# Layer 0's first adaLN columns summed by TensorE instead of GpSimd, h from x in two VectorE operations, rotary constants made in layer 0's MLP

## The chip, the cores and the metric

The kernel runs on one core of one Trainium2 chip. The metric is the time of one execution on the device in microseconds (us), the median of several runs. The engines are TensorE (PE; its weight loads are shown as PEld), VectorE (DVE), ScalarE (ACT), GpSimd (POOL) and SyncE (SP, which issues most transfers). Each engine takes its instructions in the order in which the built program holds them and waits where an operand is not there yet.

## The reference

A trunk of two layers on a sequence of 1024 tokens of 1024 features, all in fp32. Layer 0 mixes tokens by gated linear attention, layer 1 by differential attention with rotary positions; a squared-ReLU MLP follows each. Ahead of each mixer and MLP the input is normed and modulated by six vectors that depend on the condition `c` (adaLN). What the change touches:

```python
ang = positions.astype(f32)[..., None] * inv_freq
cos = jnp.cos(ang); sin = jnp.sin(ang)                      # used in layer 1
c_act = jax.nn.silu(c)
mod = c_act @ ada_w[i] + ada_b[i]                           # 1024 -> 6 x 1024
shift_t, scale_t, gate_t, shift_c, scale_c, gate_c = split(mod, 6)
h = rmsnorm(x, norm_g[i, 0]) * (1.0 + scale_t) + shift_t    # input of the mixer
q, k, v, r, a_lr = split(h @ w_in)                          # layer 0
```

## The kernel before, in words

Features lie on the 128 partitions in eight tiles k, tokens in the free dimension in two halves of 512. Every fp32 product is made of three products of rounded operands: `split` (L114 on ACT, L115 on DVE) writes a tile as `hi` plus `lo`, and `mm3` multiplies hi by hi, hi by lo and lo by hi (L118, L119, L120).

The begin works on the first half of the tokens. SP fetches x token by token (`xt`); ACT sums squares (L260) and `rsqrt_cols` makes 1/rms per token; PE transposes x into feature tiles (`tr`, L344), ACT copies them out (`xT`, L345), and PE spreads 1/rms over the partitions (`bc`, L164). DVE multiplies the two into `xn` (L346).

Only the first 2048 of 6144 adaLN columns, shift and scale of the mixer, are needed now. They come in four blocks (`blk`): 256 columns of shift and the same 256 of scale, for all eight k, as a tile `aw` of [128, 4, 2, 256] per half of the k (four buffers). The vector-matrix product is made in two steps: first acc[p, column] = sum over k of w[p, k, column] * cact[p, k], in which ACT makes the products for k = 0, 1, 2 (L332), POOL adds two of them (L334), and DVE adds the other five as chained multiply-adds (L336); then PE sums acc over the partitions, by four products with a column of ones (`st`, L356). DVE adds the bias (L360, L363: `mod`) and makes the gain (L361: `gs`). From these each block gives the h of two k tiles: ACT writes `h_hi` = g * xn + shift (L368), DVE the same in fp32 (`ht`, L369) and `h_lo` = ht - h_hi (L370). PE then takes up the products of the new h tiles with the weights of v and the gate rank (`pv`, 272 columns), q (`pq`, 512) and k (`pk`, 512); when all eight tiles are through, it transposes the rank part (`tra`, L431), on which the decay and the rest of the layer hang.

The order on each engine is set by a scheduler when the program is built, from its own estimate of the durations; `in_order` pins the transfers of the begin on SP's queue. The rotary constants (`diff_constants`, L1310 on) are made in the begin: some 25 small DVE operations that depend on each other, one sine on ACT between two table loads. They are used in layer 1 only.

Layer 0's MLP consists of an inner part, in which DVE and ACT make sums and splits of the weights (`ws`, `whi`, `wlo`) and of parts of the hidden (`sum`, `inner`), and of `outer`, which multiplies by the second matrix.

Of the kernel before, what the change touches and what calls it, by code (L numbers as in the profile page):

```python
# [10 lines left out]
F32 = mybir.dt.float32  # L11
# [4 lines left out]
AF = mybir.ActivationFunctionType  # L16
ALU = mybir.AluOpType
# [65 lines left out]
def trunk(ctx: ExitStack, tc, a, out):  # L83
    nc = tc.nc
    pe, act, dve, pool = nc.tensor, nc.scalar, nc.vector, nc.gpsimd


    const = ctx.enter_context(tc.tile_pool(name="const", bufs=1))
    wsp = ctx.enter_context(tc.tile_pool(name="wsp", bufs=5))
    wraw = ctx.enter_context(tc.tile_pool(name="wraw", bufs=2))  # L90
    hp = ctx.enter_context(tc.tile_pool(name="hp", bufs=2 * KT))
# [6 lines left out]

    dve.memset(const.tile([P, 40], F32, name="gap"), 0.0)
    ident = const.tile([P, P], F32, name="ident")  # L100
    make_identity(nc, ident)
    ones_col = const.tile([P, 1], F32, name="ones_col")
    dve.memset(ones_col, 1.0)
    colsT = const.tile([P, NROWS], F32, name="colsT")
    adabT = const.tile([P, 96], F32, name="adabT")
    cact = const.tile([P, KT], F32, name="cact")
# [54 lines left out]
    def broadcast(bc, cols, n):  # L161

        for j in range(n):
            pe.matmul(out=bc[:, j * P:(j + 1) * P], lhsT=cols[:, j:j + 1].broadcast_to([P, P]),  # L164
                      rhs=ident, start=True, stop=True)
# [86 lines left out]
    win = a["gla_w_in"][0]  # L252
    xn = [hp.tile([P, HT], F32, name="xn", tag="hhi") for _ in range(KT)]
    xT = [hp.tile([P, HT], F32, name="xT", tag="hlo") for _ in range(KT)]
# [8 lines left out]
    with tc.tile_pool(name="xa", bufs=4, reuse_waits="tile") as xa, \  # L263
# [30 lines left out]
        pe.transpose(out=st0[:, 2, 16:16 + KT], in_=pos_f, identity=ident[:KT, :KT])  # L294
        pos = pro.tile([P, KT], F32, name="pos")
        dve.tensor_copy(out=pos, in_=st0[:, 2, 16:16 + KT])
# [9 lines left out]
        pe.matmul(out=st0[:, 2, 40:42], lhsT=ones_col[:DH, :].broadcast_to([DH, P]), rhs=lp, start=True, stop=True)  # L306
        le = pro.tile([P, 2], F32, name="le")
        act.activation(out=le, in_=st0[:, 2, 40:42], func=AF.Exp)

        xt = []  # L310
        for j in range(4):
            t = xa.tile([P, D], F32, name="xt", tag="xt")
# [4 lines left out]
        token_rms(xt, pro2, ssq, rstd, pro.tile([P, D], BF16, name="junk"))  # L317
        cos, sin, neglam, gsub, cmin = diff_constants(tc, const, pro, pos, le, colsT)
        w_v0, w_q0, w_k0 = [], None, None
        aw = a["ada_w"][0][:, 0:2 * D].rearrange("(k p) (j n) -> p k j n", p=P, j=2)  # L320
        for blk in range(4):
            c0 = blk * 256
            acc = pro2.tile([P, 2, 256], F32, name="acc", tag="acc")
            for kq in range(2):
                w = pro2.tile([P, 4, 2, 256], F32, name="aw", tag="aw", bufs=4)
                for j in (1, 0):
                    in_order(nc.sync.dma_start(out=w[:, :, j, :], in_=aw[:, 4 * kq:4 * kq + 4, j, c0:c0 + 256]))
                for i in range(4):
                    k = 4 * kq + i
                    if k < 3:  # L330
                        p = acc if k == 0 else pro2.tile([P, 2, 256], F32, name="prod", tag="prod")
                        act.activation(out=p, in_=w[:, i], func=AF.Copy, scale=cact[:, k:k + 1])  # L332
                        if k:
                            pool.tensor_tensor(out=acc, in0=acc, in1=p, op=ALU.add)  # L334
                    else:
                        dve.scalar_tensor_tensor(out=acc, in0=w[:, i], scalar=cact[:, k:k + 1], in1=acc,  # L336
                                                 op0=ALU.mult, op1=ALU.add)
            if blk == 0:
                bc = mm.tile([P, HT], F32, name="bc", tag="mm")
                broadcast(bc, rstd, 4)  # L340
                for k in range(KT):
                    tr = gp2.tile([P, HT], F32, name="tr", tag="tr", bufs=2)
                    for j in range(4):
                        pe.transpose(out=tr[:, j * P:(j + 1) * P], in_=xt[j][:, k * P:(k + 1) * P], identity=ident)  # L344
                    act.copy(out=xT[k], in_=tr)  # L345
                    dve.tensor_tensor(out=xn[k], in0=xT[k], in1=bc, op=ALU.mult)  # L346
                w_v0 += gla_v(0, 0, True)
            elif blk == 1:
                w_q0 = wcols(win, 0, DK, True)
            elif blk == 2:  # L350
                w_k0 = wcols(win, 512, DK, True)
                w_v0 += gla_v(0, 1, True)
            st = gp2.tile([P, 4], F32, name="st", tag="tr", bufs=2)
            for j in (1, 0):
                for n in range(2):
                    pe.matmul(out=st[:, 2 * j + n:2 * j + n + 1], lhsT=acc[:, j, n * P:(n + 1) * P], rhs=ones_col,  # L356
                              start=True, stop=True)
            ks = slice(2 * blk, 2 * blk + 2)
            shift, scale = mod[:, 0, 0:KT][:, ks], mod[:, 0, KT:2 * KT][:, ks]
            dve.tensor_tensor(out=scale, in0=st[:, 2:4], in1=adabT[:, KT:2 * KT][:, ks], op=ALU.add)  # L360
            dve.scalar_tensor_tensor(out=gs[:, 0, ks], in0=scale, scalar=1.0, in1=colsT[:, NG_ROW:NG_ROW + KT][:, ks],  # L361
                                     op0=ALU.add, op1=ALU.mult)
            dve.tensor_tensor(out=shift, in0=st[:, 0:2], in1=adabT[:, 0:KT][:, ks], op=ALU.add)  # L363
            for k in (2 * blk, 2 * blk + 1):
                hi, lo = h[k][0]
                t = pro2.tile([P, HT], F32, name="ht", tag="ht")
                g, sh = gs[:, 0, k:k + 1], mod[:, 0, k:k + 1]
                act.activation(out=hi, in_=xn[k], func=AF.Identity, scale=g, bias=sh)  # L368
                dve.tensor_scalar(out=t, in0=xn[k], scalar1=g, scalar2=sh, op0=ALU.mult, op1=ALU.add)  # L369
                dve.tensor_tensor(out=lo, in0=t, in1=hi.bitcast(F32), op=ALU.subtract)  # L370


# [389 lines left out]
    def inner(l, h, w_o, x, early, g, sm, tp, ps, acc_tile):  # L762
# [146 lines left out]
        for n in range(8, FF // P, 2):  # L909
            for _ in pair(n):  # L910
                pass

    def outer(l, ada_todo, after, g, tp, ps, acc_tile):

# [18 lines left out]
        def load_inner(c, between=lambda: None):  # L933
# [64 lines left out]

    win = a["diff_w_in"][0]
    o = [[None, None] for _ in range(KT)]  # L1000
    x = [[None, None] for _ in range(KT)]
    x_half = ExitStack()
    with ExitStack() as g:
# [305 lines left out]
def diff_constants(tc, const, dc, pos, le, colsT):  # L1309
# [3 lines left out]
    act, dve, pool = nc.scalar, nc.vector, nc.gpsimd  # L1313
    ang = dc.tile([P, KT, 8], F32, name="ang", tag="ang", bufs=1)
    inv = np.float32(ROPE_THETA) ** (-np.arange(0, ROPE_DIM, 2, dtype=np.float32) / np.float32(ROPE_DIM))
    for f in range(8):
        dve.tensor_scalar(out=ang[:, :, f], in0=pos, scalar1=float(inv[f]), scalar2=None, op0=ALU.mult)
    magic = 1.5 * 2.0 ** 23
    cnt = dc.tile([P, KT, 8], F32, name="cnt", tag="cnt", bufs=1)

# [10 lines left out]
    dve.tensor_scalar(out=ang, in0=ang, scalar1=lim, scalar2=-lim, op0=ALU.min, op1=ALU.max)  # L1331
    arg = dc.tile([P, 2, KT, 8], F32, name="arg", tag="arg", bufs=1)
    dve.tensor_copy(out=arg[:, 0], in_=ang)
# [43 lines left out]
```

## Time and profile before

| | before |
|---|---|
| median of 3 runs | 2480.8 us (2478.12 to 2481.04) |
| the profiled execution | 2476.71 us, span 2474.9 |
| PE busy | 2385.8 us, 96% of the span |
| DVE, ACT, POOL busy | 1680.7, 990.8, 201.4 us |
| mean granted clock of TensorE | 0.988 |

Times inside the trace count from the start of the span. A busy time is the union of the spans of an engine's instructions; matmuls are pipelined, so the distance between two starts, not the duration of one, is what each costs in a row of them. A wait in brackets is the idle time of the engine just before the instruction, with what ended it.

### The profile page before, as it was taken

How to read it: one execution, taken by the hardware profiler on the slowest of the kernel's cores; microseconds unless marked ns; L12 is line 12 of the kernel's file. 1: busy time of each engine (PE TensorE's matmuls, PEld its weight loads, DVE VectorE, ACT ScalarE, POOL GpSimd, SP SyncE). 2: the span in 40 equal slices, each digit the busy share in tenths (PEclk: the TensorE clock that was granted, in tenths of full speed). 3: DMA queues.
4: the chain of work that ended last, by engine and by line, in shares of the span. 5: the costliest groups of instructions: out<-in, count | busy, mean ns of one | idle time of the engine just before them, and what ended most of it. 6: DMA issues, size and time to landing. Idle time of an engine off the chain costs nothing.

```text
span 2474.9 us, 33402 instructions
## 1 busy us (share of the span) xinstructions
PE 2385.8 (96%) x12215; PEld 2052.2 (83%) x12215; DVE 1680.7 (68%) x3191; ACT 990.8 (40%) x1969; POOL 201.4 (8%) x354
## 2 busy tenths in 40 slices
PE   6899999999999999899999999999999999999998
PEld 5788878877888888788999999987778888888887
DVE  7777777676665767774787788788676565555344
ACT  5655556443333321211555555564442333222111
POOL 2011100000000102210221111120000000000000
PEclk9899999999999999999999999999999999999999
DMA  8333353524333845651211111024523334633111
GB/s 292 116 119 107 104 169 126 155 78 123 112 102 121 308 138 170 220 163 63 73 43 35 35 35 35 25 90 133 157 81 107 117 117 129 237 109 113 63 45 69
DMA packets 270116, 286.57 MB, mean 116 GB/s; under 512 B 15546, under 2 KB 200032, under 8 KB 269952
## 3 DMA queue, kind: packets, MB, share of 16 engines
q1 hardware_dynamic: 255552, 240.24, 30.5%
q0 software_dynamic: 12992, 41.97, 5.3%
q8 instruction: 96, 1.57, 0.3%
q10 hardware_dynamic: 1408, 2.24, 0.2%
q14 instruction: 68, 0.56, 0.1%
HBM read 222.52 MB, written 61.87 MB: 115 GB/s over the span
## 4 chain that ended last, share of the span: by engine, by line
PE 72%; issue 11%; DMA 7%; DVE 6%; ACT 3%; POOL 1%; SPq 0%; DVEq 0%; POOLq 0%; ACTq 0%
PE acc L118 10%; PE acc L119 10%; PE acc L120 10%; PE acc L856 7%; PE acc L857 7%; PE acc L858 7%; DMA ada_raw<-in_ada_w 5%; PE pp L118 3%; PE pp L120 3%; PE pp L119 3%; PE at L1155 1%; PE pr L118 1%; PE pr L119 1%; PE pr L120 1%; PE bc L164 1%
## 5 line engine op out<-in xcount | busy, mean ns | idle before, releaser
L114 ACT CAST whi<-raw 128x1024 fp32r<-128x1024 f32 (+3 forms) x217 | 209.1, 965 | 495.4 <-PE acc L119 272.1
L718 DVE SCALAR_TENSOR_TENSOR x<-acc,mod,x 128x512 f32<-128x512 f32 (+1 forms) x312 | 223.0, 720 | 230.2 <-PE acc L120 226.4
L118 PE MATMUL acc<-h_hi,whi 128*128 128x512 f32 x896 | 353.0, 394 | 2.7 <-DVE x L718 2.6
L119 PE MATMUL acc<-h_lo,whi 128*128 128x512 f32 x896 | 350.5, 391 | 0.0
L120 PE MATMUL acc<-h_hi,wlo 128*128 128x512 f32 x896 | 350.4, 391 | 0.0
L115 DVE TENSOR_TENSOR wlo<-raw,whi 128x1024 fp32r<-128x1024 f32 (+3 forms) x217 | 242.8, 1120 | 72.2 <-ACT whi L114 68.4
L118 PE MATMUL acc<-hd,whi 128*128 128x512 f32 (+1 forms) x576 | 211.7, 368 | 1.2 <-DVE x L718 1.2
L119 PE MATMUL acc<-hd,whi 128*128 128x512 f32 (+1 forms) x576 | 210.7, 366 | 0.0
L120 PE MATMUL acc<-hd,wlo 128*128 128x512 f32 (+1 forms) x576 | 210.5, 366 | 0.0
L118 PEld LDWEIGHTS acc<-h_hi,whi 128*128 128x128 f32 x896 | 169.3, 189 | 37.7 <-DVE x L718 3.8
L120 PEld LDWEIGHTS acc<-h_hi,wlo 128*128 128x128 f32 x896 | 169.0, 189 | 35.2
L119 PEld LDWEIGHTS acc<-h_lo,whi 128*128 128x128 f32 x896 | 169.3, 189 | 33.5
L118 PE MATMUL pp<-whi,h_hi 128*128 128x384 f32 x512 | 182.8, 357 | 0.0
L856 PE MATMUL acc<-h_hi,whi 128*128 128x512 f32 x448 | 175.7, 392 | 0.4 <-DVE sum L876 0.4
L857 PE MATMUL acc<-h_lo,whi 128*128 128x512 f32 x448 | 175.3, 391 | 0.0
L858 PE MATMUL acc<-h_hi,wlo 128*128 128x512 f32 x448 | 174.2, 390 | 0.0
L120 PE MATMUL pp<-whi,h_lo 128*128 128x384 f32 x512 | 172.6, 337 | 0.0
L119 PE MATMUL pp<-wlo,h_hi 128*128 128x384 f32 x512 | 172.2, 336 | 0.0
L213 POOL DMA_DIRECT2D ada_raw<-in_ada_w x160 | 86.1, 539 | 968.1 <-DVE wlo L115 455.0
L218 DVE SCALAR_TENSOR_TENSOR ada_acc<-ada_raw,cact,ada_acc 128x512 f32<-128x512 f32 x140 | 104.8, 748 | 55.2 <-DMA ada_raw<-in_ada_w 53.5
L856 PE MATMUL acc<-tq,whi 128*128 128x512 f32 x336 | 132.3, 394 | 9.8 <-ACT whi L114 9.8
L858 PE MATMUL acc<-tq,wlo 128*128 128x512 f32 x336 | 132.0, 393 | 0.1
(1800 smaller groups left out, 5189.0 us busy)
## 6 DMA issues: line engine op xcount, KB each, us to landing
raw<-in_mlp_w SPq DMA_DIRECT2D x128, 512.0 KB, 4.5
ada_raw<-in_ada_w POOLq DMA_DIRECT2D x160, 256.0 KB, 3.3
inner<-hs SPq DMA_DIRECT2D x128, 256.0 KB, 3.6
hs<-inner SPq DMA_DIRECT2D x112, 256.0 KB, 2.8
x<-xs SPq DMA_DIRECT2D x64, 256.0 KB, 5.8
raw<-in_gla_w_in SPq DMA_DIRECT2D x24, 512.0 KB, 3.7
xs<-x SPq DMA_DIRECT2D x48, 256.0 KB, 2.8
raw<-in_diff_w_in SPq DMA_DIRECT2D x64, 192.0 KB, 2.9
```

What stands on the lines that cost most here:

```text
L114: act.copy(out=hi, in_=src)
L115: dve.tensor_tensor(out=lo, in0=src, in1=hi.bitcast(F32), op=ALU.subtract)
L118: pe.matmul(out=o, lhsT=lh, rhs=rh, start=start, stop=False)
L119: pe.matmul(out=o, lhsT=lh, rhs=rl, start=False, stop=False)
L120: return pe.matmul(out=o, lhsT=ll, rhs=rh, start=False, stop=stop)
L164: pe.matmul(out=bc[:, j * P:(j + 1) * P], lhsT=cols[:, j:j + 1].broadcast_to([P, P]), rhs=ident, start=True, stop=True)
L213: queue.dma_start(out=w, in_=a["ada_w"][l].rearrange("(k p) n -> p k n", p=P)[:, k:k + kk, c0:c0 + n])
L218: dve.scalar_tensor_tensor(out=acc, in0=w[:, j, :], scalar=cact[:, k + j:k + j + 1], in1=acc, op0=ALU.mult, op1=ALU.add)
L718: return dve.scalar_tensor_tensor(out=t, in0=psum, scalar=mcols(l, gate)[:, kt:kt + 1], in1=t, op0=ALU.mult, op1=ALU.add)
L856: pe.matmul(out=pt, lhsT=lh, rhs=rh, start=begin and k == 0, stop=False, skip_group_check=True)
L857: pe.matmul(out=pt, lhsT=lh, rhs=rl, start=False, stop=False, skip_group_check=True)
L858: pe.matmul(out=pt, lhsT=ll, rhs=rh, start=False, stop=k == K2 - 1, skip_group_check=True)
```

## The change

Four edits. The column sums of block 0 are made by PE alone, 8 k x 4 products with the column `cact[:, k]` as moving operand, straight from `aw`; in block 1 PE does so for k = 4 to 7, and ACT and DVE make `acc` from k = 0 to 3; in blocks 2 and 3 ACT starts `acc` with k = 0 and DVE adds the other seven. POOL has none. `xn` is gone: ACT copies `bc` to `bcs`, DVE makes `ht` = xT * g * bcs, ACT h_hi = ht + shift, and DVE h_lo = (ht + shift) - h_hi. `diff_constants` is called in `outer` of layer 0, its three work tiles come from the pool `tp` under the tag `t` that MLP tiles use, and `pos` and `le` are kept in `const` for it. A filler memset is 24 instead of 40 columns wide.

```diff
-        cos, sin, neglam, gsub, cmin = diff_constants(tc, const, pro, pos, le, colsT)
...
-            acc = pro2.tile([P, 2, 256], F32, name="acc", tag="acc")
+            by_pe, ws = (KT, 4, 0, 0)[blk], []
+            acc = pro2.tile([P, 2, 256], F32, name="acc", tag="acc") if by_pe < KT else None
...
-                    if k < 3:
-                        p = acc if k == 0 else pro2.tile([P, 2, 256], F32, name="prod", tag="prod")
-                        act.activation(out=p, in_=w[:, i], func=AF.Copy, scale=cact[:, k:k + 1])
-                        if k:
-                            pool.tensor_tensor(out=acc, in0=acc, in1=p, op=ALU.add)
+                    if k >= KT - by_pe:
+                        ws.append((w[:, i], cact[:, k:k + 1]))
+                    elif k == 0:
+                        act.activation(out=acc, in_=w[:, i], func=AF.Copy, scale=cact[:, k:k + 1])
                     else:
                         dve.scalar_tensor_tensor(out=acc, in0=w[:, i], scalar=cact[:, k:k + 1], in1=acc,
                                                  op0=ALU.mult, op1=ALU.add)
+            if acc is not None:
+                ws.append((acc, ones_col))
...
+                bcs = pro.tile([P, HT], F32, name="bcs")
+                act.copy(out=bcs, in_=bc)
...
-                    dve.tensor_tensor(out=xn[k], in0=xT[k], in1=bc, op=ALU.mult)
...
-            for j in (1, 0):
-                for n in range(2):
-                    pe.matmul(out=st[:, 2 * j + n:2 * j + n + 1], lhsT=acc[:, j, n * P:(n + 1) * P], rhs=ones_col,
-                              start=True, stop=True)
+            for i, (w, c) in enumerate(ws):
+                for m in (2, 3, 0, 1):
+                    j, n = m // 2, m % 2
+                    pe.matmul(out=st[:, m:m + 1], lhsT=w[:, j, n * P:(n + 1) * P], rhs=c,
+                              start=i == 0 and m == 2, stop=i == len(ws) - 1, skip_group_check=True)
...
-                act.activation(out=hi, in_=xn[k], func=AF.Identity, scale=g, bias=sh)
-                dve.tensor_scalar(out=t, in0=xn[k], scalar1=g, scalar2=sh, op0=ALU.mult, op1=ALU.add)
-                dve.tensor_tensor(out=lo, in0=t, in1=hi.bitcast(F32), op=ALU.subtract)
+                dve.scalar_tensor_tensor(out=t, in0=xT[k], scalar=g, in1=bcs, op0=ALU.mult, op1=ALU.mult)
+                act.activation(out=hi, in_=t, func=AF.Identity, bias=sh)
+                dve.scalar_tensor_tensor(out=lo, in0=t, scalar=sh, in1=hi.bitcast(F32), op0=ALU.add,
+                                         op1=ALU.subtract)
...
+        if l == 0:
+            rotary.extend(diff_constants(tc, const, tp, pos, le, colsT))
...
-    ang = dc.tile([P, KT, 8], F32, name="ang", tag="ang", bufs=1)
+    ang = dc.tile([P, HT], F32, name="ang", tag="t")[:, :8 * KT].rearrange("p (k f) -> p k f", f=8)
```

The scheduler moves instructions with it. PE's queue around the sums of block 0, before, from the last transposes on (`tr`); xN is a count of equal instructions:

```order
L344 MATMUL tr<-ident,xt 128x128 x8
L356 MATMUL st<-ones_col,acc 128x1 x4
L118 MATMUL pv<-whi,h_hi 128x272
L119 MATMUL pv<-wlo,h_hi 128x272
L118 MATMUL pv<-whi,h_hi 128x272
L120 MATMUL pv<-whi,h_lo 128x272
```

The same place now, as far as the sums of block 1:

```order
L346 MATMUL tr<-ident,xt 128x128 x12
L358 MATMUL st<-cact,aw 128x1 x32
L118 MATMUL pv<-whi,h_hi 128x272 x4
L119 MATMUL pv<-wlo,h_hi 128x272 x4
L120 MATMUL pv<-whi,h_lo 128x272 x4
L118 MATMUL pv<-whi,h_hi 128x272
L119 MATMUL pv<-wlo,h_hi 128x272
L120 MATMUL pv<-whi,h_lo 128x272
L118 MATMUL pv<-whi,h_hi 128x272
L119 MATMUL pv<-wlo,h_hi 128x272
L120 MATMUL pv<-whi,h_lo 128x272
L358 MATMUL st<-cact,aw 128x1 x2
```

32 calls stand between the transposes and the first product, where 4 stood; behind the last row shown come 6 more `pv`, 14 calls of L358 with `aw` and 4 with `acc`.

DVE's queue from the third block's `mod` to the fourth's, before:

```order
L360 TENSOR_TENSOR mod<-st,adabT 128x2
L363 TENSOR_TENSOR mod<-st,adabT 128x2
L361 SCALAR_TENSOR_TENSOR gs<-mod,colsT 128x2
L369 TENSOR_SCALAR ht<-xn,gs,mod 128x512 x2
L370 TENSOR_TENSOR h_lo<-ht,h_hi 128x512
L336 SCALAR_TENSOR_TENSOR acc<-aw,cact,acc 128x512
L370 TENSOR_TENSOR h_lo<-ht,h_hi 128x512
L336 SCALAR_TENSOR_TENSOR acc<-aw,cact,acc 128x512 x4
```

and now:

```order
L362 TENSOR_TENSOR mod<-st,adabT 128x2
L365 TENSOR_TENSOR mod<-st,adabT 128x2
L363 SCALAR_TENSOR_TENSOR gs<-mod,colsT 128x2
L370 SCALAR_TENSOR_TENSOR ht<-xT,gs,bcs 128x512
L115 TENSOR_TENSOR wlo<-raw,whi 128x1088
L372 SCALAR_TENSOR_TENSOR h_lo<-ht,mod,h_hi 128x512
L370 SCALAR_TENSOR_TENSOR ht<-xT,gs,bcs 128x512
L334 SCALAR_TENSOR_TENSOR acc<-aw,cact,acc 128x512 x2
L372 SCALAR_TENSOR_TENSOR h_lo<-ht,mod,h_hi 128x512
L334 SCALAR_TENSOR_TENSOR acc<-aw,cact,acc 128x512 x5
```

Five multiply-adds have become seven, and the split of the second part of the v weights (`wlo`, 128x1088) now stands in this stretch.

In layer 0's MLP the rotary operations stand on DVE ahead of the inner part's first `sum`, where before the sum came directly behind the last `h_lo`:

```order
L115 TENSOR_TENSOR h_lo<-x,h_hi 128x512
L1324 TENSOR_SCALAR ang<-pos 128x8 x8
L1329 TENSOR_SCALAR cnt<-ang 128x64
L1330 TENSOR_SCALAR cnt<-cnt 128x64
L1336 SCALAR_TENSOR_TENSOR ang<-cnt,ang 128x64 x10
L878 TENSOR_TENSOR sum<-acc,part 128x512
```

The other rotary operations follow between the next splits.

## Rows read from the trace of the kernel before

**Rows 1.** The page, part 1: busy us, share of span, count of each engine.

```profile
PE 2385.8 (96%) x12215; PEld 2052.2 (83%) x12215; DVE 1680.7 (68%) x3191; ACT 990.8 (40%) x1969; POOL 201.4 (8%) x354
```

**Rows 2.** Stretches: us; busy PE, PEld, DVE, ACT, POOL; clock; DMA share; GB/s.

```profile
20.00:30.00 10.00, 3.04 (x14) 2.53 (x12) 9.96 (x20) 8.24 (x12) 5.09 (x8) 1.00 1.02 322
...
20.40:64.30 43.90, 32.58 (x177) 28.40 (x177) 37.36 (x65) 23.63 (x38) 10.87 (x11) 0.96 0.79 265
```

**Rows 3.** Timeline, PE, 18 to 33 us: start, duration, engine, line, operation.

```profile
18.46 1.97 PE L344 MATMUL tr<-ident,xt 128*128 128x128 f32 x8
...
23.05 1.84 PE L356 MATMUL st<-ones_col,acc 128*128 128x1 f32 x8 [2.62 <-DVE arg L1336]
...
32.58 0.43 PE L118 MATMUL pv<-whi,h_hi 128*128 128x272 f32 x1
...
32.81 0.43 PE L119 MATMUL pv<-wlo,h_hi 128*128 128x272 f32 x1
```

**Rows 4.** Timeline, PE, 38 to 46 us; in brackets the idle time before.

```profile
38.56 1.02 PE L356 MATMUL st<-ones_col,acc 128*128 128x1 f32 x8
...
40.88 0.49 PE L118 MATMUL pv<-whi,h_hi 128*128 128x272 f32 x1 [1.29 <-ACT h_hi L368]
...
45.56 0.28 PE L118 MATMUL pv<-whi,h_hi 128*128 128x272 f32 x1
...
45.68 0.29 PE L119 MATMUL pv<-wlo,h_hi 128*128 128x272 f32 x1
```

**Rows 5.** Timeline, DVE: the `mod` operation of each block.

```profile
27.12 0.14 DVE L360 TENSOR_TENSOR mod<-st,adabT 128x2 f32<-128x2 f32 x1
...
39.62 0.16 DVE L360 TENSOR_TENSOR mod<-st,adabT 128x2 f32<-128x2 f32 x1 [0.55 <-PE st L356]
...
49.70 0.16 DVE L360 TENSOR_TENSOR mod<-st,adabT 128x2 f32<-128x2 f32 x1 [1.56 <-PE st L356]
...
57.20 0.16 DVE L360 TENSOR_TENSOR mod<-st,adabT 128x2 f32<-128x2 f32 x1 [1.21 <-PE st L356]
```

**Rows 6.** Timeline, DVE: chained multiply-adds, two splits, a pair of independent ones.

```profile
36.10 2.98 DVE L336 SCALAR_TENSOR_TENSOR acc<-aw,cact,acc 128x512 f32<-128x512 f32 x4
...
43.36 1.22 DVE L115 TENSOR_TENSOR wlo<-raw,whi 128x1024 fp32r<-128x1024 f32 x1
...
45.16 1.28 DVE L115 TENSOR_TENSOR wlo<-raw,whi 128x1088 fp32r<-128x1088 f32 x1
...
76.21 1.40 DVE L611 SCALAR_TENSOR_TENSOR xh<-xc,gs,bc 128x512 f32<-128x512 f32 x2
```

**Rows 7.** Two stretches at the low clock; columns as in rows 2.

```profile
41.00:44.40 3.40, 3.40 (x14) 3.21 (x15) 3.40 (x6) 2.48 (x3) 0.00 (x0) 0.50 1.09 352
...
68.30:82.00 13.70, 9.43 (x41) 7.61 (x40) 12.63 (x20) 11.30 (x21) 0.60 (x1) 0.50 0.44 153
```

**Rows 8.** Timeline, PE: the gate ranks are transposed.

```profile
64.32 0.60 PE L431 MATMUL tra<-ident,at 128*16 128x128 f32 x4
```

**Rows 9.** Timeline, DVE and POOL: rotary steps, `xn`, a split beside POOL.

```profile
12.48 1.27 DVE L1329 SCALAR_TENSOR_TENSOR ang<-cnt,ang 128x64 f32<-128x64 f32 x5
...
22.93 3.06 DVE L346 TENSOR_TENSOR xn<-xT,bc 128x512 f32<-128x512 f32 x5
...
32.13 2.96 POOL L334 TENSOR_TENSOR acc<-acc,prod 128x512 f32<-128x512 f32 x2 [2.48 <-ACT prod L332]
...
33.88 2.29 DVE L115 TENSOR_TENSOR wlo<-raw,whi 128x1024 fp32r<-128x1024 f32 x1
```

**Rows 10.** Timeline, DVE, layer 0's MLP, begin of its inner part.

```profile
553.58 0.69 DVE L876 TENSOR_TENSOR sum<-acc,part 128x512 f32<-128x512 f32 x1 [2.96 <-PE acc L858]
...
555.28 0.69 DVE L840 TENSOR_TENSOR ws<-raw 128x512 f32<-128x512 f32 x1 [1.01 <-DMA raw<-in_mlp_w]
```

**Rows 11.** SP's fourth group of column requests; column requests with us to landing.

```profile
37.17 2.73 SPq L327 DMA_DIRECT2D aw<-in_ada_w  x4
...
aw<-in_ada_w SPq DMA_DIRECT2D x16, 512.0 KB, 7.5
```

More of the change, by code (lines that the diff above doesn't have):

```diff
@@ L97, in trunk @@
     hs = dram.tile([FF // P, P, T], F32, name="hs")
-    dve.memset(const.tile([P, 40], F32, name="gap"), 0.0)
+    dve.memset(const.tile([P, 24], F32, name="gap"), 0.0)
     ident = const.tile([P, P], F32, name="ident")
@@ L252, in trunk @@
     win = a["gla_w_in"][0]
-    xn = [hp.tile([P, HT], F32, name="xn", tag="hhi") for _ in range(KT)]
     xT = [hp.tile([P, HT], F32, name="xT", tag="hlo") for _ in range(KT)]
@@ L294, in trunk @@
         pe.transpose(out=st0[:, 2, 16:16 + KT], in_=pos_f, identity=ident[:KT, :KT])
-        pos = pro.tile([P, KT], F32, name="pos")
+        pos = const.tile([P, KT], F32, name="pos")
         dve.tensor_copy(out=pos, in_=st0[:, 2, 16:16 + KT])
@@ L306, in trunk @@
         pe.matmul(out=st0[:, 2, 40:42], lhsT=ones_col[:DH, :].broadcast_to([DH, P]), rhs=lp, start=True, stop=True)
-        le = pro.tile([P, 2], F32, name="le")
+        le = const.tile([P, 2], F32, name="le")
         act.activation(out=le, in_=st0[:, 2, 40:42], func=AF.Exp)
@@ L911, in inner @@
                 pass
+    rotary = []
     def outer(l, ada_todo, after, g, tp, ps, acc_tile):
@@ L999, in trunk @@
     win = a["diff_w_in"][0]
+    cos, sin, neglam, gsub, cmin = rotary
     o = [[None, None] for _ in range(KT)]
@@ L1318, in diff_constants @@
     magic = 1.5 * 2.0 ** 23
-    cnt = dc.tile([P, KT, 8], F32, name="cnt", tag="cnt", bufs=1)
+    cnt = dc.tile([P, HT], F32, name="cnt", tag="t")[:, :8 * KT].rearrange("p (k f) -> p k f", f=8)
     def turns():
@@ L1331, in diff_constants @@
     dve.tensor_scalar(out=ang, in0=ang, scalar1=lim, scalar2=-lim, op0=ALU.min, op1=ALU.max)
-    arg = dc.tile([P, 2, KT, 8], F32, name="arg", tag="arg", bufs=1)
+    arg = dc.tile([P, HT], F32, name="arg", tag="t")[:, :16 * KT].rearrange("p (s k f) -> p s k f", s=2, f=8)
     dve.tensor_copy(out=arg[:, 0], in_=ang)
```

## The prediction

> **What bounds the kernel now.** I read the page first: PE is busy 96% of the span, so a delay that PE takes over early stays to the end unless a later wait swallows it [rows 1]. Then the busy time of the stretch the change rewrites, 20.4 to 64.3 us: PE 32.6 of 43.9 us, VectorE (DVE) 37.4, ScalarE (ACT) 23.6, GpSimd (POOL) 10.9 [rows 2]. The begin is not bound by PE: DVE is the fullest engine. Then the timeline of the two engines. The begin is four blocks of 256 columns, and each is one ring: the column sums `st` end on PE, DVE makes `mod` and `gs`, ACT and DVE make two h tiles, PE multiplies them, DVE adds up the next block's products, PE sums them. The four marks are the four `mod` operations at 27.12, 39.62, 49.70 and 57.20 us [rows 5]; the stage ends when PE transposes the gate ranks (`tra`) at 64.32 [rows 8]. I forecast these five times for the changed kernel.
>
> Two levels of TensorE's clock matter. The clock column says 1.00 in 20 to 30 us [rows 2], but the durations contradict it: eight rows of `st` take 1.84 us at 23.05 and 1.02 at 38.56, and two neighbouring `pv` products start 0.23 us apart at 32.58 and 0.12 apart at 45.56 [rows 3, 4]. So the begin runs at 1.2 GHz and the level of 2.4 comes later. It falls to 1.2 again for 41.0 to 44.4 and 68.3 to 82.0, where the column does show 0.50 [rows 7]; before the fall at 41.0 PE had run, after 38.6, only eight `st` rows and nothing until 40.88 [rows 4].
>
> **The change part by part.** *Sums by PE.* A product of a 128x128 fp32 weight with one column stands in the trace as two rows (four such calls, eight rows). Before there are 16 calls, in four groups of four; now there are 32 for block 0, 16+4 for block 1, and 4 each for blocks 2 and 3: 60, so 88 rows more. One row costs 1.84/8 = 0.23 at 1.2 GHz (starts 0.22 apart, which I use as 0.223) and 1.02/8, less the overlap of the last one, 0.121 at 2.4 [rows 3, 4]. These two are the ends of the unknown. Which one holds is a matter of the clock's level, and no stretch of before consists of such calls for long. The nearest rows are the 32 transposes, each with a 128x128 load, the last eight without a pause up to 20.43: they leave the clock at 1.2, as the `st` rows at 23.05 show [rows 3]; and the fall at 41.0 after `st` rows [rows 4, 7]. I take 1.2 for block 0.
>
> The Trainium skill, TensorE: Matmul & The Clock Gate, section "Back-to-back issue gap", gives a lone matmul of up to 64 columns a floor of about 25 ns. By that, an estimate from the page, block 0's 64 rows would take 1.6 us where the rows say 14.3, and the change would gain some 5 us. The same section says that a stream of load-multiply pairs is spaced by both, and that is what 0.121 and 0.22 per row show; the trace decides against the floor.
>
> Mark 0. The transposes end at 20.4 in both orders; I give nothing for the ACT copies that leave their neighbourhood, though up to 1 us may come. 64 x 0.223 = 14.3, so `mod` at 34.7 (before: 27.12, +7.6). In exchange DVE loses eight `xn` operations (five of them took 3.06) and the rotary chain (five steps 1.27) here [rows 9]; before, these stood between the sums and `mod`, now they are covered by PE's 14 us and are worth nothing.
>
> Mark 1. DVE after `mod`: 0.4 for `mod`, `mod`, `gs`; two `ht`, now SCALAR_TENSOR_TENSOR, 1.40 as the pair at 76.21; the weight split 1.25 (1.22 and 1.28); two `h_lo`, of the same form as that pair, 0.70 each [rows 6]. That is 4.45, and PE waits for it, because 14 of the 24 `pv` products are done by then. Left are 10 `pv` (2.3 at 0.23) and, in PE's queue, 20 calls of sums: 40 rows, 4.8 at 2.4 GHz or 8.9 at 1.2. So 34.7 + 4.45 + 2.3 + (4.8 to 8.9) = 46.3 to 50.4. The level should rise under the products and fall again under the sums; I take the middle, 48.3 (before 39.62, +8.7). DVE's three products for this block (2.2) are ready long before.
>
> Mark 2. No sums by PE here, but POOL and two ACT steps are gone, so DVE has seven chained products, four of which took 2.98: 7 x 0.745 = 5.2 [rows 6]. DVE: 0.4 + 1.4 + 0.7 + 1.25 + 0.7 + 5.2 = 9.65; four calls 0.97 and 0.1 to `mod`: 10.7, so 59.0 (before 49.70, +9.3). Before, this distance was 10.1: there the split took 2.29 beside POOL's work against 1.22 alone, and that relief is inside my figures [rows 6, 9].
>
> Mark 3. DVE: 0.4 + 0.7 + 1.25 (the split of the second `v` weights now stands behind the first `ht`) + 0.7 + 0.7 + 1.5 + 0.7 + 3.7 = 9.65, and 1.07: 69.7. Before, the distance was 7.5, since five DVE products sufficed and that split had been done a block earlier: +12.5.
>
> End. From mark 3 to `tra` before: 7.1. Now `h_hi` waits for `ht`: +0.75. PE runs dry about 4 us before mark 3's h, so I let its last products begin at 1.2 for as long as the dip of 41.0 to 44.4 lasted: 3.4 us that do half their work, +1.7 [rows 7]. `tra` at 79.3, +15.0. What follows (68.3 to 82.0, PE busy 9.4 of 13.7 at 1.2) keeps its order, and I expect it to look alike.
>
> *Rotary in the MLP.* The 10 first chained steps stand on DVE where it idled 2.96 before `sum` and 1.01 before `ws` [rows 10]. From 550.6, or from the landing of the last `hs` store whose buffer `cnt` takes over, say 552, the 10 chained steps and two ahead of them need 12 x 0.25 = 3.0 [rows 9], the eight short products ahead of those less, say 0.8: they end at 554.4 to 555.8 and push `ws` (555.28), on which PE waits, by 0 to 1. The rest falls among splits; two table loads go to ACT, where before only copies and casts stand. I take +0.5, with 0 to 2.
>
> *At nothing:* `bcs`, one ACT copy while PE still transposes (if it were late, 0.6 once); the smaller filler memset; SP's queue, whose requests stand in the same order (its risk is the rival below).
>
> Sum: +15.5. The profiled execution took 2476.7 us (span 2474.9), 4.1 less than the median 2480.8. That gives 2492.2 on its scale, 2496.3 on the median's; I say 2495.
>
> **The rivals.** *The clock rises under the sums.* For: the products that ran without a pause from 40.9 on were followed by the high level (0.12 apart at 45.56) [rows 4], and PE would have no pause here either. Against: the transposes and the fall at 41.0. With 4.2 us at the low level (19 rows) and 45 rows at 0.121: 20.4 + 4.2 + 5.4 = 30.0, marks 30.1, 40.6, 51.3, 62.0, `tra` 71.5, +7.2; with the MLP 2488.5, between 2484 and 2491.
>
> *Full clock from the start, and faster.* If 2.4 GHz came already under the transposes, they could save at most half of their 32 x 0.25 = 4.0. Then marks 24.3, 34.8, 45.5, 56.2 and `tra` 64.0: DVE's longer chain in blocks 2 and 3 eats what the first two win. Only if the stretch at 1.2 after 68.3 went too (half of 9.4) would the total be 4.8 lower: 2476. It decides only when both happen, and nothing in the rows speaks for it.
>
> *One-column products cost next to nothing.* Then PE adds no time, and DVE and the products alone set the marks: 20.5, 27.3, 37.0, 46.8, `tra` 56.3, 8.0 earlier: 2473 on the median's scale. It decides where a row is far below 0.12, and none of the L356 rows is. The skill's floor, named above, would be such a case.
>
> *SP is late.* Block 3's columns were issued at 37.17 behind a request that waits for a weight split; `aw` takes 7.5 to land [rows 11]. Now that split ends at mark 1 + 3.75 = 52, the columns land about 61, and DVE wants them at 59.0 + 3.75 = 62.8. If the landing slips by 4 or 5, mark 3 moves by 3: 2498 to 2500.
>
> **How the numbers follow.** Forecast 0.72, clock rises 0.16, SP late 0.06, full clock 0.04, products for nothing 0.02. The forecast's own range is 2489 to 2500: mark 1's 4 us, 2 for the MLP, 1 for the transposes, and 4 between profile and median. To hold 8 in 10 with the likeliest parts of the case of the rising clock I go down to 2485, and up to 2501 for a late SP. A measurement tells about 0.2% (5 us) from no change: slower means over 2485.8. The forecast and SP late are slower wholly, the rising clock three times in four: 0.90, less a little for what I missed, 0.88. Faster, below 2475.8, holds part of the last two: 0.05. The rest, 0.07, is the same.
>
> **What would show it.** Right: the L358 rows of block 0 at 0.22 apart, filling PE from 20 to 34; four `mod` at about 35, 48, 59 and 70; DVE idle for some 14 us ahead of the first; seven chained products of 5.2 in blocks 2 and 3. Wrong: L358 rows at 0.12 (first rival), a first `mod` below 28 (second or last), DVE waiting for `aw` ahead of mark 3 (third), or a wait after 64 us that swallows the delay, which I see nowhere.

## The result and the profile after

The changed kernel takes 2494.1 us, the median of 6 runs (2492.9 to 2495.9), against 2479.1 before (6 runs on the same chip, 2475.0 to 2481.0): 1.0063 times the time, with a 95% interval of 1.0050 to 1.0076, 15.0 us more. Forecast were 2495 and 2485 to 2501. The traced execution took 2493.0 us (span 2491.3), 16.3 more than the one of before.

The total agrees with the sum of the prediction, and two of its terms do not: the begin costs 4 us less, and 4 us arise where none were forecast.

The page's first part answers to [rows 1]: PE is busy 16.5 us longer, as long as the span grew (16.4).

```profile
PE 2402.3 (96%) x12303; PEld 2071.0 (83%) x12303; DVE 1674.3 (67%) x3180; ACT 986.1 (40%) x1961; POOL 189.8 (8%) x346
```

The timeline of PE in the begin (start, duration, engine, line, operation; in brackets the idle time before) answers to [rows 3, 4]:

```profile
17.68 2.84 PE L346 MATMUL tr<-ident,xt 128*128 128x128 f32 x12
20.36 10.69 PE L358 MATMUL st<-cact,aw 128*128 128x1 f32 x64
33.04 1.27 PE L118 MATMUL pv<-whi,h_hi 128*128 128x272 f32 x4 [1.99 <-ACT h_hi L371]
...
38.66 4.00 PE L358 MATMUL st<-cact,aw 128*128 128x1 f32 x28
42.51 1.85 PE L358 MATMUL st<-ones_col,acc 128*128 128x1 f32 x8
...
75.69 0.60 PE L433 MATMUL tra<-ident,at 128*16 128x128 f32 x4
```

Block 0's 64 rows fill PE for 10.7 us, not for 14.3. The stretches say why (columns as in [rows 2]; the clock stands after the five engines):

```profile
20.36:23.70 3.34, 3.34 (x33) 3.34 (x31) 0.00 (x0) 1.68 (x2) 1.60 (x6) 1.00 1.02 315
23.70:31.10 7.40, 7.35 (x36) 7.26 (x35) 0.01 (x1) 0.00 (x0) 0.00 (x0) 0.50 0.44 143
...
37.40:40.80 3.40, 3.40 (x32) 3.40 (x31) 0.26 (x1) 0.00 (x0) 0.00 (x0) 1.00 0.00 1
40.80:51.00 10.20, 8.21 (x36) 7.83 (x36) 6.19 (x11) 3.83 (x5) 0.00 (x0) 0.50 0.12 31
```

The level rises at 20.3, with the last transposes, and the sums begin at 2.4 GHz: 31 rows start 0.112 us apart. At 23.7, with PE busy without a pause, the clock falls to 1.2, and 33 rows start 0.213 apart. In block 1 the same happens at 40.8. DVE idles for 12.75 us ahead of 31.1. Its marks, against [rows 5], and the seven chained products of block 2:

```profile
31.09 0.16 DVE L362 TENSOR_TENSOR mod<-st,adabT 128x2 f32<-128x2 f32 x1 [12.75 <-PE st L358]
...
44.40 0.16 DVE L362 TENSOR_TENSOR mod<-st,adabT 128x2 f32<-128x2 f32 x1 [6.74 <-PE st L358]
...
49.07 5.47 DVE L334 SCALAR_TENSOR_TENSOR acc<-aw,cact,acc 128x512 f32<-128x512 f32 x7
54.45 1.22 DVE L115 TENSOR_TENSOR wlo<-raw,whi 128x1024 fp32r<-128x1024 f32 x1
55.76 0.16 DVE L362 TENSOR_TENSOR mod<-st,adabT 128x2 f32<-128x2 f32 x1
...
66.57 0.16 DVE L362 TENSOR_TENSOR mod<-st,adabT 128x2 f32<-128x2 f32 x1 [1.21 <-PE st L358]
```

So the marks lie 4.0, 4.8, 6.1 and 9.4 us behind those of before, and `tra` 11.4 [rows 8]. The same DVE instructions (matched by name and count) lie 10.5 behind at 230 us of before, 14.2 at 300, 13.6 just ahead of the MLP's rotary chain, 13.7 behind it, and between 13.7 and 16.6 from 600 us on.

In the MLP, DVE's timeline shows the moved chain, against [rows 10]:

```profile
565.32 2.56 DVE L1336 SCALAR_TENSOR_TENSOR ang<-cnt,ang 128x64 f32<-128x64 f32 x10
567.80 0.68 DVE L878 TENSOR_TENSOR sum<-acc,part 128x512 f32<-128x512 f32 x1
569.24 0.69 DVE L842 TENSOR_TENSOR ws<-raw 128x512 f32<-128x512 f32 x1 [0.76 <-DMA raw<-in_mlp_w]
```

The chain fills what was idle ahead of `sum`; `ws` waits for its transfer as before; PE waits 5.2 us there for `whi`, 4.8 before.

### The profile page after: what moved, and what is told of

Read it like the earlier page. It is cut to its first block, busy times and chain, and to the rows that moved or that the text cites. A ratio compares the mean times of both kernels' runs of the same rounds, so it can differ in the third digit from the quotient of the medians.

```text
span 2491.3 us, 33537 instructions
## 1 busy us (share of the span) xinstructions
PE 2402.3 (96%) x12303; PEld 2071.0 (83%) x12303; DVE 1674.3 (67%) x3180; ACT 986.1 (40%) x1961; POOL 189.8 (8%) x346
## 4 chain that ended last, share of the span: by engine, by line
PE 68%; issue 14%; DMA 7%; DVE 7%; ACT 3%; POOL 1%; SPq 0%; DVEq 0%; POOLq 0%; ACTq 0%
PE acc L118 9%; PE acc L119 9%; PE acc L120 9%; PE acc L858 7%; PE acc L860 7%; PE acc L859 7%; DMA ada_raw<-in_ada_w 5%; PE pp L118 3%; PE pp L120 3%; PE pp L119 3%; PE at L1162 1%; PE pr L118 1%; PE pr L119 1%; PE pr L120 1%; PE bc L164 1%
## 5 line engine op out<-in xcount | busy, mean ns | idle before, releaser
L858 PE MATMUL acc<-tq,whi 128*128 128x512 f32 x336 | 132.2, 393 | 10.8 <-ACT whi L114 10.8
```

The costliest lines, as they stand in the source:

```text
L858: pe.matmul(out=pt, lhsT=lh, rhs=rh, start=begin and k == 0, stop=False, skip_group_check=True)
```

## The experiments

Eight further kernels were run, and the changed one once more (e5). The table gives the number of k that PE sums itself in the four blocks with the columns on the moving side, the four `mod` and `tra` in the one traced execution, and the median; the ratio is to runs of before on the same chip, with its 95% interval.

| run | sums by PE | four `mod` | `tra` | median us (runs) | ratio |
|---|---|---|---|---|---|
| before | none | 27.1, 39.6, 49.7, 57.2 | 64.3 | 2479.1 (6) | |
| changed | 8, 4, 0, 0; 1 column | 31.1, 44.4, 55.8, 66.6 | 75.7 | 2494.1 (6) | 1.0063 (1.0050 to 1.0076) |
| e5 | the same again | 31.3, 44.6, 56.1, 66.9 | 76.0 | 2494.1 (6) | 1.0058 (1.0041 to 1.0075) |
| e1 | none; DVE seven a block | 23.8, 35.5, 47.7, 57.9 | 65.7 | 2481.5 (11) | 1.0007 (0.9998 to 1.0016) |
| e2 | none; POOL two, DVE five | 24.7, 39.4, 50.7, 60.4 | 69.8 | 2485.8 (6) | 1.0031 (1.0018 to 1.0044) |
| e4 | before, rotary moved | 25.7, 37.2, 48.2, 57.9 | 66.6 | 2480.3 (11) | 1.0008 (0.9998 to 1.0018) |
| e3 | 8, 4, 0, 0; 128 columns | 27.1, 31.8, 43.6, 53.9 | 61.7 | 2478.1 (11) | 0.9994 (0.9984 to 1.0003) |
| e6 | 8, 4, 0, 0; 64 columns | 27.9, 40.2, 52.2, 62.0 | 71.4 | 2488.5 (6) | 1.0040 (1.0025 to 1.0055) |
| e9 | 4, 4, 0, 0; 1 column | 26.3, 42.1, 53.6, 64.4 | 73.6 | 2483.9 (12) | 1.0020 (1.0010 to 1.0030) |
| e7 | 4, 4, 0, 0; 128 columns | 24.2, 32.0, 43.8, 52.5 | 60.4 | 2475.6 (12) | 0.9982 (0.9971 to 0.9992) |
| e8 | 2, 2, 0, 0; 128 columns | 22.6, 34.4, 45.2, 54.9 | 62.7 | 2478.2 (12) | 0.9994 (0.9984 to 1.0005) |

**No sums by PE.**

```diff
-            by_pe, ws = (KT, 4, 0, 0)[blk], []
+            by_pe, ws = (0, 0, 0, 0)[blk], []
```

> The changed kernel with one number different: no block's columns are summed by TensorE alone; ScalarE makes the first product and VectorE the other seven in all four blocks, and 4 one-column calls a block end the sum, as before the change. h in two operations and the rotary constants in the MLP stay. My theory: the delay of the changed kernel is made by TensorE's one-column rows in blocks 0 and 1 (20.4 to 31.0 and 37.5 to 44.4 us), while VectorE idled 12.8 us ahead of the first mod; so block 0's seven products fit into that idle time, the first mod comes at 21.4 to 24 instead of 31.1, the others at about 34, 45 and 54, tra at 62.8 instead of 75.7, and the whole is 13 us faster than the changed kernel, 2479 to 2482, a ratio of 0.9995 to the kernel before. Rival: VectorE's longer chain (h made of two chained operations, seven products) is the larger part; then the marks behind the first keep 11 to 13 us of distance, tra comes after 68 and the whole stays at 2485 or above (ratio over 1.002).

Measured: `tra` at 65.7, 2481.5 us. The first theory holds: the sums on PE, against the same sums on DVE, make 10.0 of the 11.4 us at `tra`, and 12.6 of the 15.0 in the median. 2.9 us of what was forecast (62.8) are missing. PE's timeline shows the first of it:

```profile
18.20 0.88 PE L346 MATMUL tr<-ident,xt 128*128 128x128 f32 x6
21.87 1.84 PE L358 MATMUL st<-ones_col,acc 128*128 128x1 f32 x8 [2.80 <-DVE acc L334]
```

Six transposes take 0.88, against eight in 1.97 before [rows 3]: they run at 2.4 GHz. Then PE waits 2.80 us for DVE's last product, the level falls at 21.0, within that wait, and the sums behind it run at 1.2.

**Sums as before, the rest of the change kept.**

```diff
-                    if k >= KT - by_pe:
-                        ws.append((w[:, i], cact[:, k:k + 1]))
-                    elif k == 0:
-                        act.activation(out=acc, in_=w[:, i], func=AF.Copy, scale=cact[:, k:k + 1])
+                    if k < 3:
+                        p = acc if k == 0 else pro2.tile([P, 2, 256], F32, name="prod", tag="prod")
+                        act.activation(out=p, in_=w[:, i], func=AF.Copy, scale=cact[:, k:k + 1])
+                        if k:
+                            pool.tensor_tensor(out=acc, in0=acc, in1=p, op=ALU.add)
```

> The changed kernel with the column sums of the kernel before (ScalarE makes three products, GpSimd adds two, VectorE five; TensorE 4 calls a block). Only h in two operations of VectorE and the rotary constants in the MLP remain of the change. My theory: these two parts are worth a little in the begin, where VectorE is the fullest engine: without eight xn operations and the rotary chain the first mod comes at 23 to 24 (27.1 before, 31.1 in the changed kernel); each block gives back 0.7 to 1.5 us since h_hi waits for ht and ht takes 0.70 where it took 0.5; tra at 62 to 63.5 (64.3 before): 1 to 2 us faster than the kernel before, ratio 0.9990 to 1.0000. Rival: the two chained operations cost as much per block as xn did, and tra is at 64 to 66, ratio 1.0000 to 1.0010. If the column sums by TensorE were not what made the changed kernel slower, this one would stay near 1.005.

Both expectations missed: `tra` at 69.8 instead of 62 to 66, the median 6.4 above before. The timelines of POOL and DVE show where:

```profile
27.94 6.24 POOL L333 TENSOR_TENSOR acc<-acc,prod 128x512 f32<-128x512 f32 x4 [4.63 <-ACT prod L331]
```

```profile
30.62 4.10 DVE L335 SCALAR_TENSOR_TENSOR acc<-aw,cact,acc 128x512 f32<-128x512 f32 x3 [2.59 <-POOL acc L333]
...
55.31 3.90 DVE L335 SCALAR_TENSOR_TENSOR acc<-aw,cact,acc 128x512 f32<-128x512 f32 x5 [1.30 <-POOL acc L333]
```

The scheduler let POOL make two blocks' adds in one go; DVE waits 2.59 for the first of them, and beside POOL a product takes 1.37 us (4.10 by three) where it takes 0.75 [rows 6]. With POOL the begin is 4.1 us longer than without it (e1), the median 4.3. The Trainium skill, Perfetto Trace Analysis, section "Optimizing Scalar/DVE Operations", says that GpSimd and DVE share a read port of SBUF, so that moving work between them might not help; these rows agree. With the rest of the change in place, taking POOL out is a gain; whether it is one in the order of before, whose `tra` comes at 64.3 with POOL, no run shows.

The last sentence of the expectation is not met either way: 1.0031 lies between 1.0063 and 1. With the sums of before, h in two operations and the moved rotary chain, and the order that they bring, still cost 6.4 us, and the rotary chain alone cost 0.9 (e4, below). No run has h in two operations alone, so its own price stays open.

**128 columns instead of one.**

```diff
-            st = gp2.tile([P, 4], F32, name="st", tag="tr", bufs=2)
+            st = gp2.tile([P, 4, P], F32, name="st", tag="tr", bufs=2)
...
-                    pe.matmul(out=st[:, m:m + 1], lhsT=w[:, j, n * P:(n + 1) * P], rhs=c,
+                    pe.matmul(out=st[:, m], lhsT=w[:, j, n * P:(n + 1) * P], rhs=c.broadcast_to([P, P]),
...
```

> The changed kernel, and each product of the column sums by TensorE has 128 equal columns on its moving side instead of one (the constant column is read 128 times; VectorE reads the first of the 128 results). The loads, their number and everything else stay. It asks why the clock fell at 23.7 us, 3.4 us after the one-column rows began, and at 40.8. Theory A: the level falls because rows of one column leave the multiplier idle for most of their time, though the engine's queue is never empty; then with 128 columns the level stays at 2.4 GHz through blocks 0 and 1. If a row's columns are hidden behind the next load, rows stay 0.112 apart: block 0's 64 rows take 7.2 us instead of 10.7, first mod at 27.6; block 1's 40 rows take 4.5 instead of 6.4; tra at about 70, the whole 5 to 6 us faster than the changed kernel (2488 to 2490). If columns add to the load, a row takes some 0.22 at 2.4 GHz and the first mod comes at 34 to 35. Theory B: the level follows something else (the loads, the power, the time since the begin); then it falls at 23.7 as in the changed kernel, rows are 0.112 and then 0.213 apart or more, and the time is that of the changed kernel or above.

Measured: rows 0.112 apart throughout; PE's timeline and the stretch of the sums:

```profile
19.67 10.98 PE L358 MATMUL st<-cact,aw 128*128 128x128 f32 x96
30.50 1.05 PE L358 MATMUL st<-ones_col,acc 128*128 128x128 f32 x8
31.31 0.37 PE L118 MATMUL pv<-whi,h_hi 128*128 128x272 f32 x1
```

```profile
19.70:31.30 11.60, 11.60 (x104) 11.60 (x105) 7.29 (x12) 5.23 (x7) 1.54 (x6) 1.00 0.86 263
```

All 104 rows run at 2.4 GHz, none slower for its 128 columns, and the first mod comes at 27.12, as theory A has it for block 0; that an idle multiplier is the reason, as it also says, no run shows. But the gain is 16 us, not 5 to 6. The scheduler put the sums of blocks 0 and 1 in one stretch ahead of block 0's products; the second mod follows the first by 4.7 us instead of 13.3. Two things had changed.

**64 columns**, to keep the order nearer to that of the changed kernel (the other lines as in e3).

```diff
...
-                    pe.matmul(out=st[:, m:m + 1], lhsT=w[:, j, n * P:(n + 1) * P], rhs=c,
+                    wd = 64
+                    pe.matmul(out=st[:, m, :wd], lhsT=w[:, j, n * P:(n + 1) * P], rhs=c.broadcast_to([P, wd]),
...
```

> The changed kernel with 64 equal columns instead of one on the moving side of the sums' products. With 128 two things had changed: the clock stayed at 2.4 GHz, and the planner, which gives a wider product a longer time, put all 52 sum calls of blocks 0 and 1 ahead of block 0's products. With 64 the order stays nearly that of the changed kernel: block 0's sums, 14 products or so of block 0, block 1's sums. So it shows what the clock alone is worth. Theory: 64 columns keep the level up too (rows 0.112 apart throughout); the first mod comes at 27 to 27.6 (31.1 in the changed kernel), the second at 35 to 36.5 (44.4; 31.8 with 128), tra at 65 to 67 (75.7; 61.7 with 128), the whole 9 to 11 us faster than the changed kernel, and the other 4 us of the run with 128 came by the order. Rival: what mattered in the run with 128 was the order; then marks stay within 4 us of the changed kernel's and tra is over 70. If 64 columns are too few, the level falls under the sums as with one.

Measured: the first mod near what was expected (27.9: block 0's rows stand 0.112 apart from 21.1 on), the second not (40.2). PE and the low stretch:

```profile
20.04 7.84 PE L359 MATMUL st<-cact,aw 128*128 128x64 f32 x64
29.86 0.39 PE L118 MATMUL pv<-whi,h_hi 128*128 128x272 f32 x1 [1.99 <-ACT h_hi L372]
...
32.12 6.07 PE L359 MATMUL st<-cact,aw 128*128 128x64 f32 x28
38.32 1.80 PE L359 MATMUL st<-ones_col,acc 128*128 128x64 f32 x8
```

```profile
31.40:41.60 10.20, 10.20 (x48) 10.01 (x47) 3.15 (x7) 0.02 (x1) 0.00 (x0) 0.50 0.27 88
```

After PE's wait of 1.99 us for h the level falls at 31.4, and block 1's sums run at 1.2. The theory's 9 to 11 us were 5.6 (2494.1 to 2488.5): what e3's expectation gave to the clock alone. The rival nearly holds: `tra` is over 70, and the marks lie 3.2 to 4.6 us ahead of the changed kernel's, where it gave them 4. The other 10 us of e3 came with its order, in which PE does not wait between the two blocks' sums, so that a part of them is clock again; order and width (128 for 64) are not told apart in them.

**Once more the changed kernel**, no edit.

> The changed kernel once more, unchanged. In its first trace it is 11.4 us behind at tra, 10.5 behind up to 250 us, and then 3.5 more arise in one place (TensorE waits 3.5 us where it waited 1.35, behind an adaLN transfer of the GpSimd queue that took 6.5 us instead of 4.3, and the clock falls for 3.4 us), and some 2 more behind 1000 us. Theory: the begin's 10.5 belong to the kernel and come again to within 0.5; the place at 260 us depends on how transfers happen to meet and is smaller in this execution (the traces of the other four kernels show transfers of 4.5 to 5.0 and waits of 1.6 to 1.9 there); the median over all runs of both is 11 to 15 us above before. Rival: the later 5 us belong to the change as well (it moved the phase between the transfers and the rest), and the wait of 3.5 and the fall of the clock are there again.

Measured: 2494.1 again, 13.8 above before on its chip. Up to 82 us the level rises and falls in the same places, to within 0.5; the answer to the two stretches above:

```profile
20.80:24.20 3.40, 3.40 (x33) 3.40 (x32) 0.00 (x0) 1.68 (x2) 1.42 (x5) 1.00 0.86 266
24.20:31.30 7.10, 7.08 (x34) 6.99 (x33) 0.00 (x0) 0.00 (x0) 0.00 (x0) 0.50 0.52 150
```

The place at 260 us was not there, as the theory has it, but the 3 us were: this execution is 11.7 behind at `tra`, 12.1 at 130, 13.4 at 230 and 13.9 at 300. The clock fell once more at 147, where 1.5 us are lost; from 85.6 it stood low for 10.2 us, as long as in the first execution between 88.6 and 102.2, in two pieces. The theory's "10.5 that come again" fell.

**Rotary alone**, the kernel before with this part of the change:

```diff
-        cos, sin, neglam, gsub, cmin = diff_constants(tc, const, pro, pos, le, colsT)
...
+        if l == 0:
+            rotary.extend(diff_constants(tc, const, tp, pos, le, colsT))
```

> The kernel before with the third part of the change alone: the rotary constants are made at the start of layer 0's MLP. Column sums and xn as before. Theory: in the begin VectorE is the fullest engine, and the rotary chain stands among the products and xn between 12 and 23 us, some twelve steps of 0.1 to 0.4: the first mod comes 1 to 2 us sooner than 27.12, and half or all of that reaches tra (62.5 to 64); in the MLP the chain stands in idle time and costs 0 to 0.5. The whole is 0 to 2 us faster, ratio 0.9990 to 1.0002. Rival: the first mod is held by the split of the first weights and by transposes and not by the chain, so nothing is gained in the begin, and the MLP loses up to 2 us: ratio 1.0000 to 1.0010.

Measured: the first mod 1.4 us sooner, as expected, and `tra` 2.3 later; the whole the same within its interval. The scheduler had placed other things as well (a `neglam` of 1.25 us among the products of block 1), and the level fell three times between 39 and 64 us (39.4, 49.6, 59.9) where before it fell once. Neither account is confirmed; no gain is seen.

**The count alone.**

```diff
-            by_pe, ws = (KT, 4, 0, 0)[blk], []
+            by_pe, ws = (4, 4, 0, 0)[blk], []
```

> The changed kernel with one column a product, as it is, and only the count changed: four of block 0's products are summed by TensorE instead of eight (ScalarE makes one, VectorE three). It separates the two edits of the run with 128 columns and four products, which was faster than the kernel before. Theory (rows at 0.112 until the level falls some 31 rows after the transposes, then 0.213): block 0's 40 rows take 5.4 us instead of 10.7, the first mod comes at 25 to 26, the products of block 0 start at the low level as in the changed kernel, the second mod at 36 to 39, then distances of 11.4, 10.8 and 9.1 as there: tra at 67.5 to 70.5 (75.7 in the changed kernel, 60.4 with 128 columns), the whole 2486 to 2489, ratio to before 1.0025 to 1.0040. Rival: the count is what made the other run fast and the columns add little; then tra is at 60 to 63 and the ratio under 1.0005.

Measured: the first mod at 26.3, near the forecast, the second at 42.1, 3 us behind it. In this execution the level fell at 21.7 and stayed low through block 0's products and block 1's sums:

```profile
19.50:42.10 22.60, 20.55 (x101) 19.98 (x102) 6.46 (x11) 3.53 (x5) 1.38 (x6) 0.55 0.58 177
```

Of 4.8 us won at the first mark 2.1 are left at `tra`. The traced execution took 2488.8, the second slowest of the twelve (2480.3 to 2493.0); the median is 10.2 under the changed kernel. The rival as stated (`tra` at 60 to 63, a ratio under 1.0005) is refuted, but what each edit is worth depends on where it is read. In the traces, at `tra`, the count is worth 2.1 us with one column and, from e3 to e7, 1.4 with 128, and the columns 13.2 at the same count (73.6 against 60.4). In the ratios, over all executions, e9 lies halfway: the count takes it from 1.0058 (e5) to 1.0020, the columns from there to 0.9982 (e7), some 9.4 us each, give or take 4. The traces are one execution each, of e9 a slow one and of e7 (2471.9) the second fastest of twelve, so the ratios decide: count and columns won about the same. "The columns" takes in the order that the scheduler chose with them: block 1's last 36 rows stand behind 20 products in e9, behind 10 in e7.

**Count and columns**: the diff of e3, and with it

```diff
-            by_pe, ws = (KT, 4, 0, 0)[blk], []
+            by_pe, ws = (4, 4, 0, 0)[blk], []
```

> A version that could beat both: 128 equal columns a product, and TensorE sums only four of block 0's products instead of eight (ScalarE makes one, VectorE three, in the time in which VectorE waited for the sums). 24 rows less, 2.7 us of TensorE, which in the run with 128 columns had no idle time from 17 to 44 us. Theory: the first mod at 24.3 to 25, the second at 30.5 to 31.8, tra at 59.5 to 61.5 (61.7 with eight), 0 to 2 us faster than that run, ratio to before 0.9983 to 0.9995. Rival: with fewer rows TensorE waits for h ahead of its first products, the time goes there, and tra stays at 61.5 to 63.

```profile
24.20:32.00 7.80, 6.26 (x52) 5.88 (x52) 6.34 (x12) 3.05 (x4) 0.00 (x0) 1.00 1.02 311
32.00:43.80 11.80, 11.70 (x70) 9.78 (x68) 11.01 (x18) 4.05 (x5) 0.00 (x0) 1.00 1.03 351
```

Measured: `tra` at 60.4 as expected, the second mod 0.2 us late, 2475.6 us, 0.9982 (0.9971 to 0.9992): faster than before by 4.7 us, and 18.5 us faster than the changed kernel. In the traced execution the clock stays at 2.4 from 18.0 to 72.6 us, and PE is nearly full in the second stretch.

**Fewer still**, with the diff of e3:

```diff
-            by_pe, ws = (KT, 4, 0, 0)[blk], []
+            by_pe, ws = (2, 2, 0, 0)[blk], []
```

> As the run before, with two products each of blocks 0 and 1 summed by TensorE (128 columns each), the other six by ScalarE (one) and VectorE (five). 56 rows less than with eight and four. Theory: TensorE saves 6.3 us but VectorE, full from the first mod on, gets four products more: the first mod at 22.5 to 23.5, but the first split stands ahead of ht (it ends near 23.7), so h comes at 25, the second mod at 31 to 33; from there VectorE's 10.8 a block bound it: tra at 61 to 63, the same as with eight and four within 1.5 us, ratio 0.9988 to 1.0000. Rival: TensorE's time is the bound of the begin throughout; then tra comes at 56 to 59 and the ratio is 0.9970 to 0.9985.

Measured: the first mod at 22.6 and `tra` at 62.7, as expected; the second mod at 34.4, 1.4 behind it: PE waits 3.11 us for h, and the level is low for 6.8 us from 24.7. With 128 columns too the level falls where PE waits. Fewer rows beyond e7 win nothing.

## Why the prediction came out as it did

**Mark 0: the step that failed** is "they leave the clock at 1.2, as the `st` rows at 23.05 show", and with it "I take 1.2 for block 0". Of before it is true. Its transposes stand 0.213 us apart up to the last, the `st` rows behind the pause of 2.62 us as far, and the level first rose at 34.2: the `pv` products are 0.23 apart at 32.58 [rows 3] and 0.13 apart in these two rows of before:

```profile
34.28 0.29 PE L119 MATMUL pv<-wlo,h_hi 128*128 128x272 f32 x1
34.41 0.29 PE L120 MATMUL pv<-whi,h_lo 128*128 128x272 f32 x1
```

It did not carry over. In the changed kernel the level rose with the end of the transposes, at 20.3 (20.8 in the second execution), and the sums behind are 0.112 apart. PE had no pause in the last stretch of the transposes in either kernel (before, then changed; columns as in [rows 2]; the clock column says 1.00 for both, though the rows stand 0.213 apart):

```profile
17.00:20.40 3.40, 3.40 (x15) 2.68 (x13) 3.17 (x10) 1.86 (x4) 0.53 (x1) 1.00 1.10 348
...
17.00:20.36 3.36, 3.36 (x17) 2.82 (x15) 0.32 (x2) 1.86 (x4) 0.35 (x1) 1.00 1.11 348
```

In the nine traces with h in two operations the level first rises at 17.6 to 22.5; in the two with `xn`, before and e4, at 34.2 and 32.6. Why it rose sooner without `xn` no run shows. So the 64 rows took 10.7 (31 by 0.112, 33 by 0.213) instead of 14.3, and the mark moved by 4.0, not 7.6. The two ends of a row's price, 0.121 and 0.223, were close (0.112 and 0.213); the level for the whole of block 0 was not.

**Mark 1** came 13.3 behind mark 0 (13.6 forecast), by a path a little other than the forecast one: PE waited 1.99 us for `h_hi` and from 33.04 on was never idle, so `h_lo` held nothing; 24 products, mostly at 1.2, and 40 rows, the last 36 at both levels in 5.7 us, fill the rest. **Mark 2**: 11.4 instead of 10.7. The seven products took 5.47 (5.2) and ended 10.1 behind mark 1 (9.65 forecast), and PE took up the sums 0.24 later, behind a product. The split at 54.45, 1.22, was in no term of mine (three splits fall to blocks 2 and 3, two were counted), but it ends no later than the sums beside it. **Mark 3**: 10.8 (10.7). **End**: 9.1 (9.6). `tra` came 11.4 late, not 15.0; the difference of 3.6 is that of block 0's sums, and the others cancel.

**What follows "will look alike"** failed the other way: the begin's delay grew to 14 us by 300 in both executions, in different places. In the first, 10.5 at 230 us became 14.2: an adaLN transfer took 6.5 us instead of 4.3, PE waited 3.5 us for DVE where it had waited 1.3 (the row below; the columns are the idle time in all, its times, the longest), and the clock fell for 3.4 us. In the second, 12.1 at 130 us became 13.6, where it fell at 147.

```profile
PE pv L118 <- DVE t L470: 3.5, 1, 3.5
```

That falls of the clock lie elsewhere in each execution is shown; why those of the changed kernel came to 3 or 4 us more in both is not. Between 230 and 300 us the other eight traces lose 0 to 2.2. From 600 us to the end seven of the ten lose 2.6 to 6.2 more against the one trace of before, whose time (2476.7) lies 2.4 under its own median, so no conclusion rests on that.

**The total** of +15.5 agrees with +15.0 by luck: 3.6 us too much in the begin were made up by some 4 behind it. That the mechanism was right (PE's one-column rows on the path, DVE idle for 12.75 us) e1 shows; its main term was a third too large (14.3 for 10.7).

**Rotary in the MLP**: +0.1 where +0.5 was taken (0 to 2); the chain lies in idle time, `ws` waits for its transfer.

**The rivals.** "The clock rises under the sums" gave 30.1 for mark 0, nearer to 31.1 than my 34.7, and had the wrong sign: the level rose with the first of the sums and fell under them. Its 4.2 us at the low level are worked out from no row. "Full clock from the start" and "products for nothing" fall with the first mark; the Trainium skill's 25 ns (TensorE: Matmul & The Clock Gate, "Back-to-back issue gap") is not approached by any run of rows here, and the section's other sentence, that a pair of load and multiply is spaced by both, fits only as far as the load: 128 columns cost no more than one. "SP late" fell: block 3's columns landed at 54.1 to 58.6, and DVE took them up at 59.4 without a wait.

## What to carry to other kernels

The level of the clock does not belong to an operation: behind the same transposes it was 1.2 GHz in the kernel before and 2.4 in the changed one. Where a sum hangs on it, carry both ends of the price into the forecast, as was done here for mark 1 and not for block 0. One traced execution is not the median: e9's and e7's traces put the columns at 13.2 us, the ratios at 9.4. Work moved to PE onto the path can be dear twice, by its own rows and by the clock that it leaves to the products behind it; see first which engine would idle meanwhile, and leave it what fits in its idle time (e7). A change of one operation's shape may change the scheduler's order, which here came, with the width, to 10 of 16 us (e6 and e3).

## What the runs showed of the hardware

The clock fell with PE busy for 3.34 of 3.34 us, and stayed low with PE busy for 7.35 of 7.40 (the first two stretches of the result); in the second trace it was 3.40 of 3.40 and 7.08 of 7.10. The Trainium skill, TensorE: Matmul & The Clock Gate, Part 1, ties the low level to idle time; here the trace disagrees, if busy is what the trace calls busy. The level stayed up under the same loads with 128 columns each (e3, 104 rows), and with 64 in block 0 (e6). What in the rows makes the difference is not shown.

A row of a fp32 product (two rows each) with a 128x128 load and 128 columns starts 0.112 us after the last at 2.4 GHz, like one with a single column.
